# A second feed-forward product group in seven block products instead of eight, with one more buffer for raw weights

## The chip, the cores and the metric

The kernel runs on one core of a Trainium2 chip. The metric is the time of one execution on the device in microseconds (us); smaller is better. All numbers are of this one core.

## What is computed

One layer of an encoder block on 256 rows (frames) of width 1024, in float32. `rmsnorm` scales each row; every sub-layer is normed before and after and added to `x`:

```
x = x + 0.5 * rmsnorm(swiglu(rmsnorm(x, g1), Wg1, Wu1, Wd1), p1)    # feed-forward 1
h = rmsnorm(x, gm)
merged = sigmoid(h@Wga) * attention(h) + sigmoid(h@Wgb) * spatial_gating(h)
x = x + rmsnorm(merged @ Wo, pm)                                    # the mixer
x = x + 0.5 * rmsnorm(swiglu(rmsnorm(x, g2), Wg2, Wu2, Wd2), p2)    # feed-forward 2

def swiglu(h, w_gate, w_up, w_down):
    return (silu(h @ w_gate) * (h @ w_up)) @ w_down     # 1024 -> 4096 -> 1024
```

The change is about the two feed-forwards, and there about `h @ w_gate`.

## The kernel before

**Precision.** The matmuls take their operands as float32r. Each float32 weight tile `raw` is therefore split in two parts, `hi` (a cast on ACT, L88) and `lo = raw - hi` (a subtraction on DVE, L89), and so is the transposed input `xT`. A product is three matmuls for each 128 of depth: x_hi by w_hi, x_hi by w_lo, x_lo by w_hi. A weight tile has 128 x 2048 elements, 1024 KB, and is loaded by one DMA from the SP queue (L104).

**A feed-forward** (`ffn`) goes over four blocks of 1024 of the 4096 hidden columns. In a block come the gate columns `g`, then the up columns `u`. `gate_done` takes silu of a gate result on ACT into a tile `sg` (L383); `up_done` multiplies the up result into it on DVE (L390) and puts off `turn`, which transposes the 128 x 512 tile on TensorE into a bank `hp` (L398) and splits it into `hT` (L88, L89). The down products of a finished block (`down`, L377) wait in a list `side` and are strung in between the steps of the next block, eight to a block, each of 12 matmuls for the two halves of the rows.

**Two ways to make 1024 columns.** `section` needs eight block products: 4 weight tiles, each split once and used for both halves of the 256 rows. It is made in eight steps of 12 matmuls. `fast` needs seven products by a scheme of the Strassen kind: the input and the weights are cut in four quarters, sums of the quarters are multiplied, and sums of the results give the output. It has seven steps, each with one product of 12 matmuls (L301) and a weight split of its own, so seven splits. The sums of the input (`sums`, L273 and L281) are made once in a feed-forward. The sums of the weights are four per use. With `dma` false all four are DVE additions of 128 x 2048 (`add`, L305). With `dma` true two of them are made by a second transfer that adds its data onto a loaded tile (`two`: a load from SP, then an accumulating DMA from the POOL queue, L315), and two remain DVE additions; five tiles of raw weights are then loaded in place of four. Five sums of results are DVE instructions of 128 x 512 (`mixed`, L309), and one result is copied on ACT (L322).

Before, the set `FAST1` (also `FAST2`) holds the up columns of blocks 1, 2 and 3. All gate columns are made by `section`, and the up columns run with `dma` false, since `dma` is `(b, "g") in quick`. In the mixer the columns `ga` alone are made by `fast`, with `dma` true.

**Order.** The program text gives each step's instructions and calls `tick` after it; `later(n, fn)` runs `fn` at the n-th tick. A planner decides at build time, from the program's order and from its own estimate of when inputs and buffers are there, the order of the instructions on each engine and queue. On the chip each engine and queue then works strictly in that order, with semaphore waits. So a load whose buffer is free can stand far ahead of its place in the text.

**Buffers.** `raws` has 6 buffers for raw weights and gains, `wts` 4 for `hi` and 4 for `lo`, `mid` 10 of 128 x 512, `psum` 8 banks, of which four hold the down sums `ys` through a feed-forward. `mask`, `wf`, `wfs`, `ws` and `idle` are small operands of the mixer (`idle`: of the first matmuls); before, they have places of their own (`wfs` and `ws` share the pool `aux`).

Of the kernel before, what the change touches and what calls it, by code (L numbers as in the profile page):

```python
# [15 lines left out]
F32 = mybir.dt.float32  # L16
F32R = mybir.dt.float32r
# [5 lines left out]
P = 128  # L23
# [5 lines left out]
KT = D // P  # L29
H = 8  # L30
# [4 lines left out]
NB = 4  # L35
# [2 lines left out]
HOLD = 2  # L38
WARM = 14
FORGET, SCORES, TURN = 5, 3, 3  # L40
FAST1 = {(b, "u") for b in range(1, NB)}
FAST2 = FAST1
FASTM = {"ga"}

# [2 lines left out]
def block(ctx: ExitStack, tc: tile.TileContext, a: dict, out: bass.AP):  # L47
    nc = tc.nc
    const = ctx.enter_context(tc.tile_pool(name="const", bufs=1))
    raws = ctx.enter_context(tc.tile_pool(name="raws", bufs=6))  # L50
    wts = ctx.enter_context(tc.tile_pool(name="wts", bufs=4))
    mid = ctx.enter_context(tc.tile_pool(name="mid", bufs=10))
    big = ctx.enter_context(tc.tile_pool(name="big", bufs=3))
    part = ctx.enter_context(tc.tile_pool(name="part", bufs=1))
    aux = ctx.enter_context(tc.tile_pool(name="aux", bufs=1))
    small = ctx.enter_context(tc.tile_pool(name="small", bufs=4))
    psum = ctx.enter_context(tc.tile_pool(name="psum", bufs=8, space=PSUM))

# [3 lines left out]
    def mid_tile(shape, name):  # L62
        return mid.tile(shape, F32, tag="m", name=name)


    const.tile([P, 96], F32, name="pad0")
    x = const.tile([P, NT, D], F32, name="x")
    nc.sync.dma_start(out=x[:, 0, :], in_=a["x"][0])
    xT = const.tile([P, KT, NT, 2, P], F32R, name="xT")
# [55 lines left out]
    def later(n, fn):  # L125
        pending.append([n, fn])
# [158 lines left out]
    def fast(src, name, parts, done, dma):  # L285

        def get(c, kh):
            return load(src[c, kh], f"{name}{c}{kh}")

        def lhs_x(kh, t):  # L290
            return lambda k, xs: xT[:, kh * 4 + k, t, xs, :]

        def lhs_s(i):
            return lambda k, xs: parts[0][:, i, k, xs, :]

        def product(ps, lhs, raw, nm, start):
            w = parts_of(raw, f"{name}{nm}")
            for k in range(4):
                hi, lo = [z[:, k * 512:(k + 1) * 512] for z in w]
                for q, (xs, z) in enumerate(((0, hi), (0, lo), (1, hi))):  # L300
                    nc.tensor.matmul(ps, lhsT=lhs(k, xs), rhs=z, start=start and k == 0 and q == 0,  # L301
                                     stop=k == 3 and q == 2, skip_group_check=True)

        def add(out, p, q):
            nc.vector.tensor_tensor(out=out, in0=p, in1=q, op=ALU.add)  # L305

        def mixed(nm, p, q, op):
            o = mid_tile([P, 512], f"{name}{nm}")
            nc.vector.tensor_tensor(out=o, in0=p, in1=q, op=op)  # L309
            return o  # L310

        def two(first, second):

            raw = get(*first)
            nc.gpsimd.dma_start(out=raw, in_=src[second], accum_op=ALU.add)  # L315
            return raw

        b11 = get(0, 0)
        a = bank(f"{name}A")
        product(a, lhs_x(0, 0), b11, "p1", True)  # L320
        p1 = mid_tile([P, 512], f"{name}p1")
        nc.scalar.copy(out=p1, in_=a)  # L322
        yield
        if dma:
            t1 = two((1, 0), (0, 0))
        else:
            b12 = get(1, 0)
            add(b11, b11, b12)
            t1 = b11
        c = bank(f"{name}C")  # L330
        product(c, lhs_s(0), t1, "p5", True)
        yield
        b22 = get(1, 1)
        add(b11, t1, b22)
        b = bank(f"{name}B")
        product(b, lhs_s(1), b11, "p6", True)
        u2 = mixed("u2", b, p1, ALU.add)
        w = mixed("w", c, u2, ALU.subtract)
        yield
        b21 = get(0, 1)  # L340
        product(a, lhs_x(1, 0), b21, "p2", False)
        done(0, 0, a)
        add(b11, b11, b21)
        yield
        if not dma:
            add(b12, b12, b22)
        product(c, lhs_s(3), b22, "p3", False)
        done(0, 1, mixed("y01", c, u2, ALU.subtract))
        yield
        d = bank(f"{name}D")  # L350
        product(d, lhs_s(2), two((1, 0), (1, 1)) if dma else b12, "p7", True)
        done(1, 1, mixed("y11", w, d, ALU.subtract))
        yield
        product(d, lhs_x(1, 1), b11, "p4", False)
        done(1, 0, mixed("y10", d, u2, ALU.add))
        yield
# [4 lines left out]
    def ffn(n, quick, done, before=None, after=None, first=None, within=None):  # L361


        gs, us, dn = a[f"g{n}"], a[f"u{n}"], a[f"dn{n}"]
        hTs, ys, downs, sgs = {}, {}, {}, {}

        def down(f, t, cs=(0, 1)):
            if f not in downs:
# [18 lines left out]
        def up_done(b):  # L387
            def go(t, c, y):
                h = sgs[t, c]
                nc.vector.tensor_tensor(out=h, in0=y, in1=h, op=ALU.mult)  # L390

                def turn():
                    f4 = 2 * b + c
                    if f4 not in hTs:
                        hTs[f4] = big.tile([P, 4, NT, 2, P], F32R, tag="b", name=f"hT{n}_{f4}")
                    ps = bank(f"hp{n}_{b}{t}{c}")
                    for i in range(4):
                        nc.tensor.transpose(out=ps[:, i * P:(i + 1) * P], in_=h[:, i * P:(i + 1) * P], identity=ident)  # L398
                    marks[n, f4] = split(hTs[f4][:, :, t, 0, :], hTs[f4][:, :, t, 1, :],
                                         ps.rearrange("p (i c) -> p i c", c=P))[1]  # L400
                later(2, turn)
            return go

        side, parts = [], []
        for b in range(NB):
            steps = []
            for src, kind, fn in ((gs[b], "g", gate_done(b)), (us[b], "u", up_done(b))):
                nm = f"{kind}{n}_{b}"
                if (b, kind) == (0, "g"):
                    steps.append((section(src, nm, fn, first, within) if first else section_by_tile(src, nm, fn, 4), 8))  # L410
                elif (b, kind) in quick:
                    steps.append((fast(src, nm, parts, fn, (b, "g") in quick), 7))
                else:
                    steps.append((section(src, nm, fn), 8))
            total = sum(k for _, k in steps)
            keep = HOLD if b == NB - 1 else 0
            had, gone, at = len(side) - keep, 0, 0
            for gen, _ in steps:
                for _ in gen:
                    at += 1  # L420
                    if b == 0 and at == 4 and before:
                        before()
                    if b == 0 and at == 9 and quick:
                        parts.append(sums(f"f{n}"))
                    tick()
                    while had > 0 and gone < had * at // total:
                        f = side.pop(0)
                        down(f, 0)
                        down(f, 1)
                        gone += 1  # L430
            side += range(8 * b, 8 * b + 8)
# [21 lines left out]
            tick()  # L453

    def forget():
        mask = const.tile([P, P], F32, name="mask")
        nc.sync.dma_start(out=mask, in_=a["mask"])
        wf = small.tile([P, KT, H], F32, tag="wf", name="wf", bufs=1)
        nc.sync.dma_start(out=wf, in_=a["w_f"])
        bf = small.tile([H, 1], F32, tag="bf", name="bf", bufs=1)  # L460
        nc.sync.dma_start(out=bf, in_=a["b_forget"])

        wfs = aux.tile([P, KT, P], F32R, tag="aux", name="wfs")
        idr = const.tile([P, 2, P], F32R, name="idr")
        zero = const.tile([P, 1], F32, name="zero")
        pick = const.tile([P, H], F32R, name="pick")

        cs = small.tile([P, 3, P], F32R, tag="cs", name="cs", bufs=1)
        nc.vector.memset(zero, 0.0)
        with tc.issue_after(marks[1, 6].ins):  # L470
            nc.vector.tensor_copy(out=wfs, in_=zero.unsqueeze(2).broadcast_to([P, KT, P]))
            split(wfs[:, :, 0:H], wfs[:, :, 32:32 + H], wf)
            nc.vector.tensor_copy(out=idr[:, 0], in_=ident)
            nc.vector.tensor_copy(out=idr[:, 1], in_=mask)
            nc.vector.tensor_tensor(out=pick, in0=ident[:, 0:H], in1=ident[:, 32:32 + H], op=ALU.add)
            nc.vector.tensor_copy(out=cs, in_=zero.unsqueeze(2).broadcast_to([P, 3, P]))
        later(FORGET, lambda: forget_gates(wfs, bf, zero, cs))
        return cs, idr, pick
# [91 lines left out]
    def mixer(turn_in):  # L570
# [21 lines left out]
        columns(a["w_ga"], "ga", ga_done)  # L592


        ws = aux.tile([P, H, P], F32, tag="aux", name="ws")
        nc.vector.memset(ws[64:128, :, 0:64], 0.0)
        nc.sync.dma_start(out=ws[0:64], in_=a["w_s"][0:64])
        nc.sync.dma_start(out=ws[64:128, :, 64:128], in_=a["w_s"][64:128, :, 64:128])
# [76 lines left out]
        return turn  # L675


    idle = const.tile([P, 512], mybir.dt.bfloat16, name="idle")
    nc.vector.memset(idle, 0.0)
    warm = bank("warm")  # L680
    for _ in range(WARM):
# [120 lines left out]
```

## Time and profile before

| what | value |
|---|---|
| time before, median of 3 runs | 749.5 us (749.47 to 750.47) |
| the profiled execution's own time | 749.68 us |
| its span, first to last instruction | 747.9 us |
| TensorE (PE) busy | 732.6 us, 98% of the span, 3434 matmuls |
| DVE, ACT, POOL busy | 564.9, 390.4, 14.9 us |
| mean granted TensorE clock | 0.996 |

An engine's busy time is the time in which at least one of its instructions ran. PEld is TensorE's loading of the stationary operand, which overlaps its matmuls. DMA shares are shares of the core's 16 DMA engines. The profile adds 1.8 us around the span to reach the execution's own time.

### The profile page before, as it was taken

To read this page: it belongs to the slowest core of one execution; us is meant where nothing else is said; L and a number is where in the kernel's file an instruction comes from. 1 tells how busy PE (TensorE), PEld (TensorE's weight loads), DVE (VectorE), ACT (ScalarE), POOL (GpSimd) and SP (SyncE) were. 2 spreads that over 40 slices of the span, in tenths; PEclk is the share of its full clock that TensorE was granted. 3 is DMA by queue.
4 is the path that set the end of the run, shared out by engine and by line. 5 is a ranking of instruction groups with operands and counts; after the bars stand their busy time and mean duration, and the time that the engine had idled before them with its cause. 6 is when DMAs were issued, how large, how long until landed. Compare 5 with 4: busy or idle time off the path is not lost.

```text
span 747.9 us, 8563 instructions
## 1 busy us (share of the span) xinstructions
PE 732.6 (98%) x3434; PEld 605.9 (81%) x3434; DVE 564.9 (76%) x587; ACT 390.4 (52%) x406; POOL 14.9 (2%) x22
## 2 busy tenths in 40 slices
PE   7999999999999999999999999999999999999996
PEld 4888888888887877889888888878888888888785
DVE  5964798689479876769898756978489868947963
ACT  3853465456446463856774434754446435635631
POOL 0000000000000000000001000100000000000000
PEclk9999999999999999999999999999999999999999
DMA  8964167328516835873475625466417733841601
GB/s 333 393 260 174 57 230 301 143 73 341 205 57 222 322 129 192 288 200 98 166 276 212 242 96 225 139 241 240 170 59 275 285 112 126 325 168 57 250 3 57
DMA packets 23127, 144.77 MB, mean 194 GB/s; under 512 B 3312, under 2 KB 3568, under 8 KB 6576
## 3 DMA queue, kind: packets, MB, share of 16 engines
q1 hardware_dynamic: 22800, 142.13, 51.4%
q0 software_dynamic: 288, 2.10, 1.6%
q8 instruction: 27, 0.44, 0.2%
q14 instruction: 12, 0.10, 0.0%
HBM read 143.17 MB, written 1.05 MB: 193 GB/s over the span
## 4 chain that ended last, share of the span: by engine, by line
PE 89%; DVE 6%; ACT 1%; issue 1%; POOL 1%; DMA 1%; SPq 0%; POOLq 0%; DVEq 0%; ACTq 0%
PE g L225 22%; PE y L377 21%; PE u L225 9%; PE qk L204 4%; PE gb L225 3%; PE sv L225 3%; PE qk L205 2%; PE hp L398 2%; PE v L225 2%; PE u_2D L301 1%; PE u_1D L301 1%; PE wo L225 1%; PE u_3D L301 1%; PE u_1C L301 1%; PE u_2C L301 1%; PE u_2A L301 1%
## 5 line engine op out<-in xcount | busy, mean ns | idle before, releaser
L225 PE MATMUL g<-hi_g,xT 128*128 128x512 f32 x512 | 165.4, 394 | 0.7 <-ACT xT L88 0.7
L377 PE MATMUL y<-hi_d,hT 128*128 128x512 f32 x512 | 146.2, 391 | 0.0
L225 PEld LDWEIGHTS g<-hi_g,xT 128*128 128x128 f32 x512 | 96.9, 189 | 21.3 <-ACT xT L88 1.3
L377 PEld LDWEIGHTS y<-hi_d,hT 128*128 128x128 f32 x512 | 95.8, 188 | 19.6
L89 DVE TENSOR_TENSOR lo_g<-raw_g,hi_g 128x2048 fp32r<-128x2048 f32 (+1 forms) x50 | 75.0, 1519 | 41.5 <-ACT hi_g L88 41.1
L225 PE MATMUL g<-lo_g,xT 128*128 128x512 f32 x256 | 100.6, 393 | 1.1 <-DVE lo_g L89 1.1
L89 DVE TENSOR_TENSOR lo_d<-raw_d,hi_d 128x2048 fp32r<-128x2048 f32 x32 | 73.2, 2288 | 37.6 <-ACT hi_d L88 37.5
L88 ACT CAST hi_d<-raw_d 128x2048 fp32r<-128x2048 f32 x32 | 61.2, 1912 | 44.8 <-PE g L225 8.6
L377 PE MATMUL y<-lo_d,hT 128*128 128x512 f32 x256 | 80.9, 392 | 0.0
L88 ACT CAST hi_g<-raw_g 128x2048 fp32r<-128x2048 f32 (+1 forms) x50 | 62.8, 1292 | 32.3 <-PE u L225 9.3
L225 PE MATMUL u<-hi_u,xT 128*128 128x512 f32 x192 | 60.6, 391 | 0.0
L225 PEld LDWEIGHTS g<-lo_g,xT 128*128 128x128 f32 x256 | 48.5, 189 | 12.0 <-DVE lo_g L89 2.2
L305 DVE TENSOR_TENSOR raw_u<-raw_u,raw_u 128x2048 f32<-128x2048 f32 x24 | 55.0, 2292 | 0.8
L377 PEld LDWEIGHTS y<-lo_d,hT 128*128 128x128 f32 x256 | 47.8, 188 | 9.4
L383 ACT ACTIVATE sg<-g 128x512 f32<-128x512 f32 x32 | 18.8, 598 | 60.5 <-PE g L225 60.5
L204 PE MATMUL qk<-xT,hi_qk 128*128 128x512 f32 x128 | 46.5, 404 | 0.0
L225 PEld LDWEIGHTS u<-hi_u,xT 128*128 128x128 f32 x192 | 36.0, 188 | 7.4
L88 ACT CAST hi_u_3p<-raw_u 128x2048 fp32r<-128x2048 f32 x14 | 26.6, 1914 | 26.0 <-DVE raw_u L305 17.4
L89 DVE TENSOR_TENSOR lo_u_3p<-raw_u,hi_u_3p 128x2048 fp32r<-128x2048 f32 x14 | 32.0, 2287 | 9.4 <-ACT hi_u_3p L88 9.4
L225 PE MATMUL u<-lo_u,xT 128*128 128x512 f32 x96 | 37.4, 389 | 0.0
L88 ACT CAST hi_u_2p<-raw_u 128x2048 fp32r<-128x2048 f32 x14 | 26.9, 1918 | 20.1 <-DVE raw_u L305 9.5
L88 ACT CAST hi_u_1p<-raw_u 128x2048 fp32r<-128x2048 f32 x14 | 26.8, 1917 | 20.1 <-DVE raw_u L305 9.5
(289 smaller groups left out, 1292.4 us busy)
## 6 DMA issues: line engine op xcount, KB each, us to landing
raw_u<-in_u SPq DMA_DIRECT2D x32, 1024.0 KB, 4.8
raw_d<-in_dn SPq DMA_DIRECT2D x32, 1024.0 KB, 4.8
raw_g<-in_g SPq DMA_DIRECT2D x30, 1024.0 KB, 4.8
raw_qk<-in_w_qk SPq DMA_DIRECT2D x8, 1024.0 KB, 4.8
raw_ga<-in_w_ga SPq DMA_DIRECT2D x5, 1024.0 KB, 4.8
raw_v<-in_w_v SPq DMA_DIRECT2D x4, 1024.0 KB, 4.8
raw_sv<-in_w_sv SPq DMA_DIRECT2D x4, 1024.0 KB, 4.8
raw_u<-in_w_u SPq DMA_DIRECT2D x4, 1024.0 KB, 4.7
```

Source lines behind the costliest of these rows:

```text
L88: return [nc.scalar.copy(out=hi, in_=src), nc.vector.tensor_tensor(out=lo, in0=src, in1=hi.bitcast(F32), op=ALU.subtract)]
L89: nc.vector.tensor_tensor(out=lo, in0=src, in1=hi.bitcast(F32), op=ALU.subtract)]
L204: nc.tensor.matmul(ps, lhsT=hi, rhs=xT[:, k], start=k == 0, stop=False, skip_group_check=True)
L205: nc.tensor.matmul(top, lhsT=lo, rhs=xT[:, k, :, 0, :], start=False, stop=k == KT - 1, skip_group_check=True)
L225: nc.tensor.matmul(ps, lhsT=xT[:, kh * 4 + k, t, xs, :], rhs=v, start=kh == 0 and k == 0 and q == 0, stop=kh == 1 and k == 3 and q == 2)
L301: nc.tensor.matmul(ps, lhsT=lhs(k, xs), rhs=z, start=start and k == 0 and q == 0, stop=k == 3 and q == 2, skip_group_check=True)
L305: nc.vector.tensor_tensor(out=out, in0=p, in1=q, op=ALU.add)
L377: nc.tensor.matmul(ys[t][c], lhsT=hTs[f // 4][:, f % 4, t, xs, :], rhs=w[:, c * 512:(c + 1) * 512], start=f == 0 and q == 0, stop=f == NF ...
L383: nc.scalar.activation(out=sg, in_=y, func=AF.Silu)
L398: nc.tensor.transpose(out=ps[:, i * P:(i + 1) * P], in_=h[:, i * P:(i + 1) * P], identity=ident)
```

## The change

- `(2, "g")` joins the set: the gate columns of block 2 of both feed-forwards are made by `fast`. For block 2 `dma` becomes true, for the gate and for the up columns.
- `raws` has 7 buffers in place of 6, `mid` 9 in place of 10. `aux` goes; `wfs` and `ws` take a raw buffer each while they live, `mask`, `wf` and `idle` a buffer of `mid`.
- In `fast`, the third product `p3` now stands ahead of the addition `b11 + b21` and of `b12 + b22`.
- `turn` of the up results is put off by 3 ticks in place of 2 in blocks 1 and 2.
- The down products start two steps later in a block and are then spaced more closely.

```
-FAST1 = {(b, "u") for b in range(1, NB)}
+FAST1 = {(b, "u") for b in range(1, NB)} | {(2, "g")}
...
-    raws = ctx.enter_context(tc.tile_pool(name="raws", bufs=6))
+    raws = ctx.enter_context(tc.tile_pool(name="raws", bufs=7))
...
-    mid = ctx.enter_context(tc.tile_pool(name="mid", bufs=10))
+    mid = ctx.enter_context(tc.tile_pool(name="mid", bufs=9))
...
-    aux = ctx.enter_context(tc.tile_pool(name="aux", bufs=1))
...
-    const.tile([P, 96], F32, name="pad0")
+    const.tile([P, 32], F32, name="pad0")
...
         done(0, 0, a)
+        yield
+        product(c, lhs_s(3), b22, "p3", False)
         add(b11, b11, b21)
-        yield
         if not dma:
             add(b12, b12, b22)
-        product(c, lhs_s(3), b22, "p3", False)
...
+        early = [b for b in range(NB - 1) if (b, "u") in quick]
...
-                later(2, turn)
+                later(3 if b in early else 2, turn)
...
-                    while had > 0 and gone < had * at // total:
+                    while had > 0 and gone < had * max(0, at - 2) // (total - 2):
...
-        mask = const.tile([P, P], F32, name="mask")
+        mask = mid_tile([P, P], "mask")
...
-        wf = small.tile([P, KT, H], F32, tag="wf", name="wf", bufs=1)
+        wf = mid_tile([P, KT, H], "wf")
...
-        wfs = aux.tile([P, KT, P], F32R, tag="aux", name="wfs")
+        wfs = raws.tile([P, 2 * KT, P], F32R, tag="raw", name="wfs")[:, 0:KT]
...
-        ws = aux.tile([P, H, P], F32, tag="aux", name="ws")
+        ws = raws.tile([P, 2 * H, P], F32, tag="raw", name="ws")[:, 0:H]
...
-    idle = const.tile([P, 512], mybir.dt.bfloat16, name="idle")
+    idle = mid.tile([P, 512], mybir.dt.bfloat16, tag="m", name="idle")
```

## Rows read from the trace of the kernel before

**Rows 1.** The page: span, busy time of each engine

```profile
span 747.9 us, 8563 instructions
PE 732.6 (98%) x3434; PEld 605.9 (81%) x3434; DVE 564.9 (76%) x587; ACT 390.4 (52%) x406; POOL 14.9 (2%) x22
```

**Rows 2.** Chain that ended last, blocks 1 and 2: start us, us, engine, line

```profile
97.95 2.72 PE y L377 x12
...
123.88 2.73 PE g L225 x12
126.61 0.44 PE hp L398 x4
...
157.00 2.72 PE u_2A L301 x12
```

**Rows 3.** Busy time by stage: us, then PE, PEld, DVE, ACT, POOL, clock, DMA

```profile
123.88:188.35 64.47, 64.47 (x294) 53.32 (x293) 50.90 (x33) 33.53 (x24) 0.00 (x0) 1.00 0.52 195
157.00:188.00 31.00, 31.00 (x145) 25.58 (x144) 29.58 (x22) 19.28 (x13) 0.00 (x0) 1.00 0.69 264
188.35:218.75 30.40, 30.40 (x138) 25.17 (x137) 18.21 (x10) 12.22 (x10) 0.00 (x0) 1.00 0.39 142
218.00:240.00 22.00, 21.66 (x98) 17.55 (x97) 19.93 (x14) 14.04 (x9) 0.00 (x0) 1.00 0.38 133
306.00:341.00 35.00, 35.00 (x218) 31.18 (x217) 25.29 (x44) 22.09 (x39) 1.92 (x2) 1.00 0.85 249
```

**Rows 4.** Waits of PE, whole span: us in total, times, longest us

```profile
PE u_3C L301 <- DVE u_3w L309: 0.7, 2, 0.3
```

**Rows 5.** Groups by line and shape: xcount, busy us, mean ns

```profile
L89 DVE TENSOR_TENSOR lo_u_2p<-raw_u,hi_u_2p 128x2048 fp32r<-128x2048 f32 x14 | 31.9, 2289 | 1.8 <-ACT hi_u_2p L88 1.8
L88 ACT CAST hi_u_2p<-raw_u 128x2048 fp32r<-128x2048 f32 x14 | 26.9, 1918 | 20.1 <-DVE raw_u L305 9.5 <-PE u_2B L301 7.0 <-PE y L377 2.9
```

**Rows 6.** Timeline of DVE around the start of block 2

```profile
92.25 2.29 DVE L89 TENSOR_TENSOR lo_d<-raw_d,hi_d 128x2048 fp32r<-128x2048 f32 x1 [2.60 <-ACT hi_d L88]
...
113.62 2.28 DVE L89 TENSOR_TENSOR lo_g<-raw_g,hi_g 128x2048 fp32r<-128x2048 f32 x1
...
121.74 0.69 DVE L390 TENSOR_TENSOR sg<-u_1y,sg 128x512 f32<-128x512 f32 x1
122.90 2.29 DVE L89 TENSOR_TENSOR lo_g<-raw_g,hi_g 128x2048 fp32r<-128x2048 f32 x1 [0.47 <-ACT hi_g L88]
```

**Rows 7.** Timeline of DVE in the up columns of block 3

```profile
227.86 2.28 DVE L305 TENSOR_TENSOR raw_u<-raw_u,raw_u 128x2048 f32<-128x2048 f32 x1
230.06 0.69 DVE L309 TENSOR_TENSOR u_3u<-u_3B,u_3p 128x512 f32<-128x512 f32 x1
230.67 2.28 DVE L89 TENSOR_TENSOR lo_u_3p<-raw_u,hi_u_3p 128x2048 fp32r<-128x2048 f32 x1
232.87 0.69 DVE L309 TENSOR_TENSOR u_3w<-u_3C,u_3u 128x512 f32<-128x512 f32 x1
```

**Rows 8.** DMA queues and issues: packets, MB, share; KB each, us to landing

```profile
q1 hardware_dynamic: 22800, 142.13, 51.4%
q0 software_dynamic: 288, 2.10, 1.6%
...
raw_u<-in_u SPq DMA_DIRECT2D x32, 1024.0 KB, 4.8
...
raw_ga<-in_w_ga POOLq DMA_DIRECT2D x2, 1024.0 KB, 8.4
```

**Rows 9.** Timeline of POOL: the accumulating transfers of `ga`

```profile
315.72 1.05 POOL L315 DMA_DIRECT2D raw_ga<-in_w_ga  x1 [30.16 <-DMA raw_ga<-in_w_ga]
331.00 0.87 POOL L315 DMA_DIRECT2D raw_ga<-in_w_ga  x1 [14.23 <-DVE s_qk L214]
```

**Rows 10.** Timeline of the SP queue: a small operand of the mixer

```profile
58.23 0.43 SPq L457 DMA_DIRECT2D mask<-in_mask  x1
```

## The prediction

> **What bounds the kernel now.** I read the page first, then the chain of waits, then busy time by stage, then PE's own waits, then the timelines of DVE, POOL and SP around block 2. The page shows PE busy for 732.6 of 747.9 us [rows 1]. The chain shows why in the feed-forwards: it runs from one product to the next on PE, 2.72 us for each 12 matmuls, with 0.44 us for each transposed tile between them [rows 2]. By stage, block 2 of the first feed-forward lasts 64.47 us and PE is busy in all of it, while DVE has 50.90 and ACT 33.53 [rows 3]. So in that block a product less on PE is 2.72 us less, as long as nothing else becomes the last to come. PE's waits in the feed-forwards' blocks are one of 0.3 us in each, in block 3 [rows 4].
>
> **The product taken out.** Gate of block 2 goes from eight steps to seven, in each of two feed-forwards. The block had 8 + 7 + 8 = 23 steps of 2.72 and four tiles of 0.44, 64.3 us by the sum against 64.47 measured; it becomes 22 steps, 61.6 by the sum, 61.75 from the measured length. Worth 2 x 2.72 = **5.44 us**. The matmuls keep their shape, and the existing `fast` products have the same 2.72 as the section's [rows 2].
>
> **What DVE gets for it.** In a section a split serves two steps, in `fast` one: 7 splits in place of 4, so 3 more of 2.29 [rows 5], of which about 2.24 count, since neighbours overlap a little (32 or 33 instructions sum to 52.4 by their durations and to 50.90 in the window, [rows 3]). Five sums of results come in, 0.69 each and 0.61 from start to start [rows 7]. The additions of raw weights come out even: up had four on DVE, now gate and up have two each. So 50.90 + 6.7 + 3.2 = **60.8 us of DVE work in 61.75 us**, 98%. ACT gets three casts of 1.92 [rows 5] and a copy of a result (below 0.7 by its size, as the sums): 33.53 + 6.4 = 40 of 61.75, no bound.
>
> Can DVE run at 98%? The densest stretch without a PE wait is the up half of this block: 29.58 of 31.00, 95.4% [rows 3]. At that density 60.8 us of work take 63.7, which is 2.0 more than PE leaves. What hides it is the lead with which DVE enters the block: its last product of block 1 is done at 122.43, PE starts block 2 at 123.88, and the first gate split was done at 115.90 [rows 2, 6]. The new spacing puts five in place of four down steps beside block 1's up products (after steps 9, 11, 12, 14, 15), which gives DVE 2.72 us more there, so it comes about 1.45 + 2.72 = 4.2 us ahead. After the block the gate of block 3 is a section, where DVE has 18.21 of 30.40 to do [rows 3] and recovers. 4.2 covers 2.0. I therefore put no steady loss here, but an allowance for the first three steps: gate's first three products come with no down step between them, and three late `turn`s need banks of the same four that the products use, so a transposed tile's split (one 0.6 us instruction, behind at most one split of 2.29) can hold PE. The cost per block lies between 0 and 2.0 (the lead gone altogether); I take 0.6, the one small instruction, **+1.2 us** in all.
>
> **A rule against it.** The block's rows show PE busy in 64.47 of 64.47, with PEld, the loading of its stationary operand, at 53.32, 83% [rows 3]. The Trainium skill (Perfetto Trace Analysis, Identifying the Most-Contended Engine) says that matmul busy time is no good measure of TensorE's headroom, that its load time is, and that the engine with the highest share is the one to relieve. By it DVE at 98% would be the engine to relieve, and less work on PE would give nothing: the second rival below, about 747.3, where the rows give 744.6. The trace speaks for the rows as far as it goes: a chain that stays on PE through the block.
>
> **Transfers.** Each of gate and up now loads five tiles and adds two accumulating transfers: 14 loads and 4 accumulations in block 2 in place of 12 loads. A load is 2.84 us of all 16 engines (142.13 MB in 51.4% of 747.9 us; 1024 KB of it), an accumulation 6.0 (2.10 MB in 1.6%, two of them) [rows 8]. That is 39.8 + 24.0 = 63.8 us in a block of 61.75; it fits only because loads run ahead into block 1 and on into block 3, where shares are 0.39 to 0.52 [rows 3]. How far ahead: the second gate tile takes the buffer of block 1's third down tile. That one's split ended at 94.54, 3.4 us before its down product began at 97.95 [rows 2, 6]; in the new spacing this product starts 8 steps and two transposed tiles, 22.6 us, ahead of block 2. So the buffer is free at -26.0 us, the load lands after 4.8, POOL issues for 1.05, the addition lands 8.4 later [rows 8, 9]: ready at -11.7. Its split is due at -1.0 (the second product starts at +3.2; cast 1.92 and subtraction 2.29 before it). 10.7 us to spare, so nothing on the path. Behind the waiting instruction on POOL stand only the next accumulations; the norms' POOL work comes after block 3. In the mixer, `ga` has the same pattern: one POOL issue came 30.16 us after the instruction before it, at the landing of its load, and PE was busy for all 35.00 us around both, at a DMA share of 0.85 [rows 3, 9].
>
> **The third product moved ahead.** In block 3 the addition at 227.86 (2.28 us, b11 + b21) stands in front of `u_3u`, the split of the third product and `u_3w`, for which PE waits [rows 4, 7]. With the split ahead, and a fourth down step beside these products, 0.34 each should go: **-0.68 us** (bounds 0 and 0.68).
>
> **The rest, at nothing.** `turn` one step later leaves its first down product, also two steps later, one step more than before; it costs only if a bank or a `mid` buffer is short. `mask` and `wf` can take `mid` buffers as early as 58.23, where `mask` is loaded now [rows 10], and keep them to the mixer: seven of nine left in the first feed-forward, where block 2 holds at most four `sg` and three sums. The seventh raw buffer is spent on `wfs` or `ws` in the mixer (six left, as now) and is what carries the transfers above.
>
> **Sum.** 749.5 - 5.44 - 0.68 + 1.2 = **744.6 us**. The terms come from an execution of 749.68 (span 747.9), 0.2 above the median; they are small enough to be taken off the median as they are. Own range of this case: 743.4 (no allowance) to 746.5 (allowance 1.6 per block).
>
> **Rivals.**
> 1. *DVE sets the pace of block 2.* For it: 98% is above any stretch seen, and in the block 3 stretch where PE did wait DVE stood at 19.93 of 22.00, 90.6% [rows 3]. Against it: the lead. With the lead not usable and 95.4%, the block takes 63.7, 0.8 less than now: 749.5 - 1.5 - 0.7 = 747.3. At 90.6% it takes 67.1, 2.6 more: 749.5 + 5.3 - 0.7 = 754.1. It turns to a loss below 94.3% (60.8 / 64.47).
> 2. *The accumulated tile comes late* (the other side). For it: a chain of 14.25 us where a plain load has 4.8, in order on POOL, at a DMA load of a full block. Against it: 10.7 us to spare. If the buffer came free only at the split of block 1's last up product (it starts two steps and a transposed tile, 5.9 us, ahead of block 2; its split ends some 2 us before), at about -8 us, the tile were ready at +6.2, its split at +10.4 against +3.2: 7.2 us lost per block, 749.5 + 2 x (7.2 - 2.72) - 0.7 = 757.8. It decides from 10.7 + 2.7 = 13.4 us later than worked out.
> 3. *Too few `mid` buffers in the first feed-forward* (two kept by `mask` and `wf`), so only the second gains: 749.5 - 2.72 - 0.7 + 0.6 = 746.7. For it: the early load; against: the count above.
>
> **How the numbers follow.** First case 0.60. Rival 1 0.24 (0.10 faster, 0.09 within 0.2%, 0.05 slower), rival 2 0.11 (0.01 within, 0.10 slower), rival 3 0.05 (0.04 faster, 0.01 within). 0.2%, 1.5 us, is about what a measurement of this kernel tells from no change. Faster 0.74, same 0.11, slower 0.15. The range goes from 742.8, a little below the case without any allowance, to 750.5, which takes in rival 3 and the upper densities of rival 1; what is left out is below 2 in 10.
>
> **What would show it.** Right: 3410 matmuls; two steps fewer, block 2 at 61.7 to 63 us in both feed-forwards; DVE above 95% in it; PE's wait on `u_3w` gone; accumulated tiles landed 5 us or more before their split. Wrong: PE idle in block 2 ended by a `lo` split or a sum (rival 1), by a raw tile or an L315 landing (rival 2), or by `hp` and `sg` in the first feed-forward alone (rival 3).

## The result, and the profile after

The changed kernel takes 762.9 us (median of four runs, 761.8 to 764.2) against 749.75 before: ratio 1.017, interval 1.0158 to 1.0182. It is 13 us slower, where 744.6 and "faster" were forecast; the time lies outside the range. Its profiled execution took 763.53 us.

The page of the kernel after, its head and its DMA queues (queue: packets, MB, share of 16 engines):

```profile
span 761.8 us, 8586 instructions
...
PE 736.1 (97%) x3410; PEld 605.9 (80%) x3410; DVE 582.4 (76%) x603; ACT 400.7 (53%) x414; POOL 21.9 (3%) x30
...
q1 hardware_dynamic: 23376, 146.32, 51.4%
q0 software_dynamic: 1440, 10.49, 7.2%
...
raw_g<-in_g POOLq DMA_DIRECT2D x4, 1024.0 KB, 10.6
raw_u<-in_u POOLq DMA_DIRECT2D x4, 1024.0 KB, 11.6
```

The 24 matmuls are gone (3410 in place of 3434), yet PE's busy time rose from 732.6 us [rows 1] to 736.1. An accumulating transfer lands 10.6 (gate) or 11.6 us (up) after its issue, in the median of four each, where the forecast took 8.4 [rows 8].

Busy time by stage of the kernel after: blocks 1 and 2 of the first feed-forward, block 2 of the second (us, then PE, PEld, DVE, ACT, POOL, granted clock, DMA share):

```profile
59.72:124.14 64.42, 64.42 (x293) 53.43 (x292) 47.90 (x31) 31.39 (x23) 1.02 (x1) 1.00 0.51 176
124.14:195.19 71.05, 65.65 (x281) 53.00 (x280) 59.96 (x41) 40.46 (x29) 2.63 (x3) 0.95 0.81 264
596.26:666.57 70.31, 65.39 (x282) 52.85 (x280) 59.40 (x41) 40.47 (x29) 2.24 (x3) 0.95 0.82 264
```

Block 2 lasts 71.05 and 70.31 us, where it lasted 64.47 [rows 3] and should have shrunk to 61.75. Two things are new in it: PE stands still for 5.4 us (71.05 - 65.65), and PE's busy time itself is 3.9 us over 61.75, at a mean granted clock of 0.95. PE's own waits say where (us in total, times, longest):

```profile
PE u_2B L300 <- DVE lo_u_2p L88: 3.7, 2, 1.8
PE u_2B L300 <- ACT hi_u_2p L87: 3.5, 2, 1.8
...
PE g_2A L300 <- ACT hi_g_2p L87: 2.7, 2, 1.6
```

`u_2B` is the product p6 of block 2's up; PE stands still before its first and before its second matmul, right behind p5 (`u_2C`). PE's timeline there, and DVE's at the split of t1, the accumulated tile that p5 uses:

```profile
162.64 0.39 PE L300 MATMUL u_2C<-hi_u_2p,parts_f 128*128 128x512 f32 x1
164.78 0.49 PE L300 MATMUL u_2B<-hi_u_2p,parts_f 128*128 128x512 f32 x1 [1.75 <-ACT hi_u_2p L87]
167.11 0.79 PE L300 MATMUL u_2B<-lo_u_2p,parts_f 128*128 128x512 f32 x1 [1.83 <-DVE lo_u_2p L88]
```

```profile
157.71 2.29 DVE L88 TENSOR_TENSOR lo_u_2p<-raw_u,hi_u_2p 128x2048 fp32r<-128x2048 f32 x1 [4.73 <-ACT hi_u_2p L87]
```

The wait on `u_3w` of before [rows 4] is gone. The chain of waits through that place (start us, us, what):

```profile
135.18 2.21 DVE lo_d L88
137.39 0.02 issue
137.40 4.80 DMA raw_u<-in_u
...
142.73 12.94 DMA raw_u<-in_u
...
155.77 1.92 ACT hi_u_2p L87
...
159.92 0.69 DVE g_2y L308
160.60 2.21 DVE raw_u L304
162.81 0.02 issue
162.83 1.91 ACT hi_u_2p L87
164.74 0.02 issue
164.76 2.30 DVE lo_u_2p L88
167.07 0.04 issue
167.11 5.06 PE u_2B L300 x11
```

The chain is to be read upwards from the last line. PE waits for the split of p6's weights; that waits for a cast, the cast for the addition `b11 = t1 + b22`, and that addition is queued on DVE behind the split of t1 at 157.71, which waits for t1's cast and so for its accumulation (12.94 us from issue to landing). POOL could issue that only at 142.73, when t1's plain load had landed, and this load could start only when a split of a down tile gave its buffer back at 137.39, 13.3 us *after* the block had begun. The last line shows the third thing: 11 matmuls take 5.06 us, where a product of 12 took 2.72 [rows 2]. The granted clock in the stretches before, during and after that product:

```profile
164.00:167.10 3.10, 0.49 (x1) 0.19 (x1) 2.34 (x2) 3.10 (x3) 0.00 (x0) 0.84 0.98 243
167.10:172.20 5.10, 5.09 (x12) 4.02 (x13) 4.36 (x2) 3.04 (x2) 0.00 (x0) 0.50 0.77 262
172.20:175.30 3.10, 3.10 (x13) 2.49 (x13) 3.09 (x3) 1.91 (x1) 0.00 (x0) 0.88 0.40 169
```

0.50 is the lower of the clock's two levels, 1.2 GHz, right behind PE's two standstills of 1.75 and 1.83 us.

### The profile page after: what moved, and what is told of

Read it like the earlier page. It is cut to its first block, busy times and chain, and to the rows that moved or that the text cites. A ratio compares the mean times of both kernels' runs of the same rounds, so it can differ in the third digit from the quotient of the medians.

```text
span 761.8 us, 8586 instructions
## 1 busy us (share of the span) xinstructions
PE 736.1 (97%) x3410; PEld 605.9 (80%) x3410; DVE 582.4 (76%) x603; ACT 400.7 (53%) x414; POOL 21.9 (3%) x30
## 3 DMA queue, kind: packets, MB, share of 16 engines
q0 software_dynamic: 1440, 10.49, 7.2%
## 4 chain that ended last, share of the span: by engine, by line
PE 66%; DVE 13%; DMA 9%; ACT 5%; issue 4%; POOL 1%; SPq 0%; POOLq 0%; DVEq 0%; ACTq 0%
PE g L224 15%; PE y L377 14%; PE u L224 9%; DMA raw_u<-in_u 5%; DMA raw_g<-in_g 4%; PE qk L203 3%; PE gb L224 3%; PE sv L224 3%; DVE raw_u L304 2%; DVE lo_u_1p L88 2%; PE qk L204 1%; PE u_3D L300 1%; PE wo L224 1%; PE u_3C L300 1%; PE u_2D L300 1%
## 5 line engine op out<-in xcount | busy, mean ns | idle before, releaser
L224 PE MATMUL g<-hi_g,xT 128*128 128x512 f32 x384 | 125.0, 396 | 0.5 <-ACT xT L87 0.5
L224 PEld LDWEIGHTS g<-hi_g,xT 128*128 128x128 f32 x384 | 73.1, 190 | 16.3 <-ACT xT L87 1.3
L224 PE MATMUL g<-lo_g,xT 128*128 128x512 f32 x192 | 75.8, 395 | 1.1 <-DVE lo_g L88 1.1
L88 DVE TENSOR_TENSOR lo_g<-raw_g,hi_g 128x512 fp32r<-128x512 f32 (+1 forms) x42 | 56.6, 1370 | 14.3 <-ACT hi_g L87 14.1
L87 ACT CAST hi_g<-raw_g 128x512 fp32r<-128x512 f32 (+1 forms) x42 | 47.5, 1175 | 34.7 <-PE u L224 12.8
L377 PEld LDWEIGHTS y<-lo_d,hT 128*128 128x128 f32 x256 | 48.1, 189 | 11.4 <-DVE lo_d L88 1.3
L304 DVE TENSOR_TENSOR raw_u<-raw_u,raw_u 128x2048 f32<-128x2048 f32 x20 | 45.8, 2288 | 0.4
L224 PEld LDWEIGHTS g<-lo_g,xT 128*128 128x128 f32 x192 | 36.5, 190 | 9.4 <-DVE lo_g L88 2.2
L88 DVE TENSOR_TENSOR lo_u_1p<-raw_u,hi_u_1p 128x2048 fp32r<-128x2048 f32 x14 | 32.0, 2284 | 14.8 <-ACT hi_u_1p L87 14.8
L88 DVE TENSOR_TENSOR lo_u_2p<-raw_u,hi_u_2p 128x2048 fp32r<-128x2048 f32 x14 | 32.0, 2285 | 13.4 <-ACT hi_u_2p L87 13.4
L87 ACT CAST hi_g_2p<-raw_g 128x2048 fp32r<-128x2048 f32 x14 | 26.6, 1918 | 27.6 <-DVE raw_g L304 19.1
L87 ACT CAST hi_u_2p<-raw_u 128x2048 fp32r<-128x2048 f32 x14 | 26.5, 1904 | 21.2 <-DMA raw_u<-in_u 13.3
## 6 DMA issues: line engine op xcount, KB each, us to landing
raw_g<-in_g POOLq DMA_DIRECT2D x4, 1024.0 KB, 10.6
raw_u<-in_u POOLq DMA_DIRECT2D x4, 1024.0 KB, 11.6
```

Source lines behind the costliest of these rows:

```text
L87: return [nc.scalar.copy(out=hi, in_=src), nc.vector.tensor_tensor(out=lo, in0=src, in1=hi.bitcast(F32), op=ALU.subtract)]
L88: nc.vector.tensor_tensor(out=lo, in0=src, in1=hi.bitcast(F32), op=ALU.subtract)]
L224: nc.tensor.matmul(ps, lhsT=xT[:, kh * 4 + k, t, xs, :], rhs=v, start=kh == 0 and k == 0 and q == 0, stop=kh == 1 and k == 3 and q == 2)
L377: nc.tensor.matmul(ys[t][c], lhsT=hTs[f // 4][:, f % 4, t, xs, :], rhs=w[:, c * 512:(c + 1) * 512], start=f == 0 and q == 0, stop=f == NF ...
```

## The experiments

Two theories were set against each other. **T**: the accumulated tiles come too late. **V**: VectorE (DVE) is too full. All kernels are the changed one with the edit shown; `...` marks what is left out of an edit or a view, and a line number is one of the run's own kernel. e2 to e5 and e8 leave sums out and serve to measure time alone. The table has the median, the ratio to the runs of the kernel before beside it (their medians lie between 749.75 and 750.65 us) with its interval, and the length of blocks 1 and 2 together in either feed-forward in the profiled execution (from the first gate matmul of block 1 to that of block 3, read from PE's timeline). The profiled execution of e3 is its fastest (751.54 us), that of e8 its slowest (752.40), so their block lengths do not stand for their medians.

| kernel | us | ratio to before | blocks 1 + 2, us |
|---|---|---|---|
| before | 749.75 | 1 | 129.41, 129.42 |
| after | 762.89 | 1.0170 (1.0158 to 1.0182) | 135.47, 134.77 |
| e1_gate8 | 749.78 | 0.9994 (0.9985 to 1.0003) | 128.95, 128.92 |
| e2_noacc | 746.98 | 0.9959 (0.9945 to 0.9972) | 127.43, 127.40 |
| e3_noadd | 755.91 | 1.0066 (1.0044 to 1.0089) | 128.34, 131.05 |
| e4_neither | 744.80 | 0.9931 (0.9918 to 0.9945) | 126.33, 126.38 |
| e5_plain | 747.78 | 0.9969 (0.9960 to 0.9979) | 127.42, 127.45 |
| e6_alldve | 768.61 | 1.0246 (1.0231 to 1.0262) | 137.61, 137.78 |
| e7_pool | 785.65 | 1.0475 (1.0441 to 1.0509) | 148.26, 148.13 |
| e8_accgate | 749.34 | 0.9996 (0.9982 to 1.0009) | 130.08, 128.77 |
| e9_fill | 760.79 | 1.0140 (1.0125 to 1.0156) | 134.80, 133.86 |
| c1_own2 | 747.50 | 0.9965 (0.9953 to 0.9978) | 127.43, 127.47 |
| c2_own2w3 | 780.89 | 1.0421 (1.0392 to 1.0449) | 132.82, 131.33 |
| c3_own2b1 | 743.12 | 0.9909 (0.9886 to 0.9931) | 123.72, 123.76 |

**e1_gate8: the other edits alone**

```
-FAST1 = {(b, "u") for b in range(1, NB)} | {(2, "g")}
+FAST1 = {(b, "u") for b in range(1, NB)}
```

> The kernel after, but the gate of block 2 in eight products again (its up in seven, with four loads and four additions on VectorE, no accumulating transfer in block 2). Buffers, the later turn and the moved p3 stay as after. If the loss lies in the seven products of the gate and the transfers that come with them, the other edits together cost next to nothing: 748.5 to 750.5 us. If the smaller edits (ten to nine working tiles, the first step's moves, the later turn) carry part of it: 752 us or more.

749.78 us, no difference from before that can be measured. Buffers, the later `turn` and the moved p3 carry none of the loss. Blocks 1 and 2 are 0.46 us shorter, all of it in block 1, which is what one transposed tile takes (0.44 us, [rows 2]): by the later `turn` one tile fewer falls into these two blocks, and nothing is won in the whole.

**e2_noacc, e3_noadd, e4_neither: without the accumulations, without the additions, without both**

The first hunk is e2's edit, the other two are e3's, and e4 has all three.

```
-            nc.gpsimd.dma_start(out=raw, in_=src[second], accum_op=ALU.add)
+            if name == "ga":
+                nc.gpsimd.dma_start(out=raw, in_=src[second], accum_op=ALU.add)
...
-        add(b11, t1, b22)
+        if name == "ga" or not dma:
+            add(b11, t1, b22)
...
-        add(b11, b11, b21)
+        if name == "ga" or not dma:
+            add(b11, b11, b21)
```

> The kernel after without the four accumulating transfers of block 2 in each feed-forward stage's gate and up: the tiles of p5 and p7 hold one addend only, everything else is issued as after. Late transfers (theory T): both stretches without PE's work and the half-clock matmuls behind them go, 2 x (5.4 + 3.4) = 17.6 us less, so 744 to 748 us. VectorE too full (theory V): it has the same instructions to do in a block of 61.7 us, so most of the loss stays: 756 us or more. Both in part: 749 to 755 us.

> The kernel after without VectorE's two additions of raw weights in each seven-product stage of block 2 (ahead of p6 and of p4): p6 and p4 get weights that lack the second addend. VectorE has 4 x 2.3 = 9 us less to do in each block 2. Theory V: 744 to 748 us. Theory T: the accumulated tiles land as late as after, only the 2.3 us of one addition in the chain behind a landing goes per wait, at most 2 x 2 x 2.3 = 9 us with the clock's part: 754 to 760 us.

> Both left out: no accumulating transfer and no addition of raw weights in block 2. Theories T and V both: no stall in block 2, 743 to 746 us, which is what two products less per kernel can give. If it stays above 750 us, the loss lies in neither and in what is left: the order of the splits, the buffers, the later turn.

Without the accumulations 747.0, without the additions 755.9, without both 744.8. T's numbers held in the first two, and the common one in the third. Against V: with all of DVE's work and no accumulation the stalls on `u_2B` are gone. What DVE's four additions per block cost when no tile is waited for is e2 less e4, 2.2 us, 1.1 per block (c3_own2b1, below, has a block 2 without this cost). The 7 us of e3 must not be put down to DVE's load: its edit also cuts p6 loose from t1 (p6 takes the first loaded tile as it is), so it shortens just the chain shown above.

**e5_plain: a second transfer of the same size that does not add**

```
-            nc.gpsimd.dma_start(out=raw, in_=src[second], accum_op=ALU.add)
+            if name == "ga":
+                nc.gpsimd.dma_start(out=raw, in_=src[second], accum_op=ALU.add)
+            else:
+                nc.gpsimd.dma_start(out=raw, in_=src[second])
```

> The kernel after, but the second transfer of each accumulated tile of block 2 is a plain one (it writes over the first instead of adding to it, so p5 and p7 get weights that lack the first addend). Same queue, same bytes, same waits, same buffers. If the tiles are late because their buffers come free late and two transfers stand in a row: 757 to 763 us. If the accumulation itself makes the transfer long (10.6 to 13 us against about 5 us of a plain one): 746 to 751 us.

747.8 us: the same buffers, queue and bytes, and the loss is gone. The landing of the two kinds, from the DMA issues of this run, and POOL's issue for the up's first such tile:

```profile
raw_g<-in_g POOLq DMA_DIRECT2D x4, 1024.0 KB, 6.4
raw_u<-in_u POOLq DMA_DIRECT2D x4, 1024.0 KB, 6.5
...
raw_ga<-in_w_ga POOLq DMA_DIRECT2D x2, 1024.0 KB, 10.1
```

```profile
140.36 0.54 POOL L317 DMA_DIRECT2D raw_u<-in_u  x1 [19.51 <-DMA raw_u<-in_u]
```

`ga`, which still accumulates, takes 10.1; block 2's transfers, without the addition, 6.4 to 6.5, in the kernel after 10.6 to 11.6. The issue comes nearly as late as in the kernel after, 17.4 us behind the block's start (140.36 - 122.98) where it was 18.6 (142.73 - 124.14). So the late buffer alone would have been borne; the 4 to 5 us more per transfer make of it a tile that comes too late.

**e6_alldve: all sums of block 2 on DVE**

```
-                    steps.append((fast(src, nm, parts, fn, (b, "g") in quick), 7))
+                    steps.append((fast(src, nm, parts, fn, False), 7))
```

> The kernel after with all eight sums of raw weights of a block 2 on VectorE, from four plain loads per stage: no accumulating transfer. VectorE gets 4 x 2.3 = 9.1 us more in each block 2, about 70 us of work for a block of 61.7 us. Theory V (VectorE sets the pace as soon as it is over the block): 2 x (8 to 10) us of stall over the 745 us of no stall, with the clock's part 762 us or more. If its lead at the block's start and its slack behind it cover most of that: 748 to 756 us.

768.6 us: V's number. Block 2 of the first feed-forward, and ACT's timeline at one of its casts:

```profile
124.62:197.78 73.16, 66.45 (x281) 53.16 (x280) 66.87 (x44) 41.37 (x30) 0.00 (x0) 0.95 0.48 173
```

```profile
132.59 3.70 ACT L87 CAST hi_g_2p<-raw_g 128x2048 fp32r<-128x2048 f32 x2 [3.35 <-DVE raw_g L304]
```

The DMA share has dropped to 0.48 and DVE has 66.87 us to do, more than the 61.75 that PE needs. PE's longest wait (2.6 us on `g_2B` in each block 2) ends with a cast, and ACT stood idle before that cast for a sum of DVE (second fence). So V is a true limit, and 4.6 us of DVE work per stage are the price of avoiding the two accumulations in this way; but it is not what slowed the kernel after, whose DVE has two sums fewer per stage.

**e7_pool: the sums for p4 and p7 on GpSimd**

The edit of e6_alldve, and:

```
-        def add(out, p, q):
-            nc.vector.tensor_tensor(out=out, in0=p, in1=q, op=ALU.add)
+        def add(out, p, q, eng=nc.vector):
+            eng.tensor_tensor(out=out, in0=p, in1=q, op=ALU.add)
...
-        add(b11, b11, b21)
+        add(b11, b11, b21, nc.gpsimd if name.endswith("_2") else nc.vector)
...
-            add(b12, b12, b22)
+            add(b12, b12, b22, nc.gpsimd if name.endswith("_2") else nc.vector)
```

> As the run before it, but in block 2 the sums for p4 and p7 are made by GpSimd, so VectorE has just what it has in the kernel after (two sums per stage) and there are four plain loads per stage instead of five with two accumulating transfers. Theory T: without accumulating transfers the stalls go, 745 to 749 us, faster than before. Theory V: 755 us or more. A third way: GpSimd's sums are long (5 us or more each) or hold up VectorE's own while they run; then p4 or p7 waits: 752 to 760 us.

785.7 us: T's number failed, and so did the third way's upper bound of 760, though DVE held up by GpSimd is what the trace shows. The timelines of GpSimd (first line) and of DVE (the others) in one place of block 2:

```profile
136.04 4.61 POOL L304 TENSOR_TENSOR raw_g<-raw_g,raw_g 128x2048 f32<-128x2048 f32 x1 [9.47 <-DVE lo_g_2p L88]
```

```profile
136.48 6.32 DVE L88 TENSOR_TENSOR lo_g_2p<-raw_g,hi_g_2p 128x2048 fp32r<-128x2048 f32 x1
142.72 2.28 DVE L88 TENSOR_TENSOR lo_d<-raw_d,hi_d 128x2048 fp32r<-128x2048 f32 x1
```

GpSimd adds from 136.04 to 140.65. The split that DVE begins at 136.48 takes 6.32 us, not 2.28: what is left of GpSimd's addition (4.17) and then its own length, 6.45 by the sum. It stood still until GpSimd was done. In the four places of this block DVE's instruction beside such a sum is 2.7 to 4.4 us longer than its like elsewhere. The Trainium skill (SBUF — State Buffer, SBUF: two separate sides) says that the two engines share a pair of ports that one instruction holds for its whole length, and that a DVE instruction with two SBUF inputs is locked out by a GpSimd one that reads SBUF. This trace agrees, with 6.32 us in place of 2.28. A sum moved to GpSimd therefore costs DVE more here than the 2.3 us of making it itself.

**e8_accgate: the accumulations of the gate alone**

```
-            nc.gpsimd.dma_start(out=raw, in_=src[second], accum_op=ALU.add)
+            if name[0] == "g":
+                nc.gpsimd.dma_start(out=raw, in_=src[second], accum_op=ALU.add)
```

> The kernel after with the accumulating transfers of block 2's gate, but without those of its up (p5 and p7 of the up get one addend only). If the up's tiles, of which the chain of waits names the longest, cause most: 748 to 752 us. If the gate's transfers set off the loss (everything behind them on VectorE and ScalarE is late, too): 755 us or more.

749.3 us. Without the up's accumulations the kernel after is 13.6 us faster. The gate's cost about 2.4 us (749.3 against 747.0 without any), and their wait is PE's longest in this run:

```profile
PE g_2A L300 <- ACT hi_g_2p L87: 3.7, 2, 2.0
```

**e9_fill: PE kept at work in the stall**

```
+        kept = [None, None]
...
+            if nm == "p6" and name[0] == "u" and name.endswith("_2"):
+                for i in range(8):
+                    nc.tensor.matmul(ps, lhsT=lhs(0, 0), rhs=kept[0][:, 0:512], start=True, stop=True,
+                                     skip_group_check=True)
...
+            kept[:] = w
```

> The kernel after with eight more matmuls (3.1 us, of values that the next start overwrites) on PE just ahead of p6 of block 2's up, where PE stands still for 3.6 us in all. The stall itself stays as long; only PE is kept at work in it. If the half clock behind the stall (the 11 matmuls of p6 take 5.06 us instead of 2.72, and some more at a granted clock of 0.84 to 0.88) is a consequence of PE's idle time: 2 x 3.4 = 6.8 us less, about 756 us. If the clock falls for another reason, or the added matmuls come to stand behind the stall: 763 to 769 us.

760.8 us: 2 us less where 6.8 were expected. PE's timeline at p6 and at the up's last step, and busy time by stage, of the stretch between the two and of the whole block 2, in this run:

```profile
162.29 1.98 PE L300 MATMUL u_2B<-hi_u_2p,parts_f 128*128 128x512 f32 x8
164.11 0.39 PE L307 MATMUL u_2B<-hi_u_2p,parts_f 128*128 128x512 f32 x1
166.25 0.50 PE L307 MATMUL u_2B<-lo_u_2p,parts_f 128*128 128x512 f32 x1 [1.75 <-DVE lo_u_2p L88]
...
187.55 0.47 PE L307 MATMUL u_2D<-hi_u_2p,xT 128*128 128x512 f32 x1 [1.71 <-DVE u_2y L315]
```

```profile
163.91:187.55 23.64, 20.18 (x90) 16.11 (x89) 23.64 (x16) 15.33 (x9) 0.00 (x0) 1.00 0.89 325
123.23:193.61 70.38, 64.72 (x290) 52.48 (x288) 61.53 (x43) 40.37 (x29) 2.62 (x3) 1.00 0.85 279
```

The clock's part of the expectation came true: with only one standstill left (1.75 us; the added matmuls filled 1.8 of 3.6), the granted clock stays at 1.00. PE's busy time, 64.72 us with the 1.8 of added matmuls in it, is 2.8 below that of the kernel after. But PE then runs into a new wait of 1.7 us at `u_2D`, for a result sum of DVE. The last fence's first line tells why: from the late split on, DVE is busy for 23.64 of 23.64 us. It had stood idle 4.4 us for the accumulated tile, and in a block that it nearly fills there is no place to make them up. In the kernel after there is no wait at `u_2D`: there the slow p6 seems to have hidden this second queue.

**c1_own2: two buffers of their own for the accumulated tiles**

```
-    raws = ctx.enter_context(tc.tile_pool(name="raws", bufs=7))
+    raws = ctx.enter_context(tc.tile_pool(name="raws", bufs=5))
+    acc = ctx.enter_context(tc.tile_pool(name="acc", bufs=2))
...
-            raw = get(*first)
+            if name.endswith("_2"):
+                raw = acc.tile([P, 2048], F32, tag="acc", name=f"acc_{name}{first[0]}{first[1]}{second[0]}")
+                nc.sync.dma_start(out=raw, in_=src[first])
+            else:
+                raw = get(*first)
```

> The kernel after with two buffers of their own for the accumulated tiles of block 2, and five raw buffers for all else instead of seven shared ones: the first load of the up's p5 tile can then go as soon as the gate's p5 tile is split, about 28 us before it is due, where load and accumulation need 5 + 13 = 18 us. Theory T (late by the chain load, accumulation, split, not by the transfers' sum): the stalls in block 2 go, 746 to 750 us, if five buffers do for the rest. If the rest needs six or seven: its waits come in other places, 752 us or more. If the transfers' sum (DMA engines full, accumulation at 6.0 us of engine time per MB) sets it: 758 us or more.

747.5 us, faster than both kernels, at the same number of buffers. The accumulations are not shorter on the whole (gate 11.4 against 10.6, up 9.8 against 11.6); they start earlier. POOL's timeline, and the landing times:

```profile
130.87 0.88 POOL L319 DMA_DIRECT2D acc_u<-in_u  x1 [62.06 <-ACT hT L88]
151.81 0.88 POOL L319 DMA_DIRECT2D acc_u<-in_u  x1 [20.06 <-DMA acc_u<-in_u]
```

```profile
acc_g<-in_g POOLq DMA_DIRECT2D x4, 1024.0 KB, 11.4
...
acc_u<-in_u POOLq DMA_DIRECT2D x4, 1024.0 KB, 9.8
```

The up's first accumulation is issued 7.4 us after the block's start (130.87 - 123.42), not 18.6 (142.73 - 124.14). So the sum of the transfers, with the same accumulations, is not what sets the loss. In block 2 of this run PE is busy in 62.34 of 63.01 us and DVE in 58.45.

**c2_own2w3: the space taken from the split weights instead**

```
+    acc = ctx.enter_context(tc.tile_pool(name="acc", bufs=2))
-    wts = ctx.enter_context(tc.tile_pool(name="wts", bufs=4))
+    wts = ctx.enter_context(tc.tile_pool(name="wts", bufs=3))
```

The accumulated tiles come from `acc`, as in c1_own2; `raws` stays at 7.

> The same two own buffers, with all seven raw buffers kept and the space taken from the split weights (three pairs of hi and lo instead of four). Theory T as before: no stall by transfers in block 2. The split weights' lead falls from three products to two, so VectorE's bursts (98% busy in block 2) show sooner: 747 to 752 us if a lead of 5.4 us does, 755 us or more if not.

780.9 us, the expectation's case "755 us or more", and far beyond that bound. Little of it lies in block 2: in the first feed-forward that lasts 64.08 us, but block 1 68.74, and from block 3 to the second feed-forward it is 309.4 us where it was 288.6 before. PE's waits in this run include 4.4 us in the mixer and 1.6 on `u_3w` in each feed-forward. The kernel needs the fourth pair of split weights nearly everywhere; raw buffers it can spare.

**c3_own2b1: block 1's gate in seven products as well**

The edit of c1_own2, and:

```
-FAST1 = {(b, "u") for b in range(1, NB)} | {(2, "g")}
+FAST1 = {(b, "u") for b in range(1, NB)} | {(1, "g"), (2, "g")}
...
-            if name.endswith("_2"):
+            if name[-2:] in ("_1", "_2"):
```

> The kernel with two own buffers for accumulated tiles (the 747.5 us one), and the gate of block 1 in seven products too, its and its up's p5 and p7 tiles accumulated in the same two buffers: two more products less, and eight more accumulating transfers in the kernel. If a block in which VectorE has 98% to do costs nothing as long as the tiles are there, as block 2 in the run before: 2 x 2 us less, 743 to 745 us. If VectorE's lead pays for one such block alone (its work of 60.8 us was measured as 58.5 inside the block of 63.0, the rest done ahead), the second one stalls: 748 to 756 us. If the accumulating transfers of two blocks in a row (8 x 6.0 us of engine time) are too many: its waits end at their landing, 752 us or more.

743.1 us, 0.9909 of before (0.9886 to 0.9931). Blocks 1 and 2 of the first feed-forward, then block 1 and 2 of the second:

```profile
62.03:123.87 61.84, 61.84 (x282) 51.03 (x280) 56.71 (x39) 37.53 (x27) 3.50 (x4) 1.00 0.89 288
123.87:185.75 61.88, 61.88 (x282) 51.13 (x280) 58.00 (x41) 40.69 (x29) 3.50 (x4) 1.00 0.90 304
521.98:583.81 61.83, 61.83 (x281) 51.01 (x280) 56.72 (x39) 37.54 (x27) 3.52 (x4) 1.00 0.88 282
583.81:645.74 61.93, 61.93 (x282) 51.11 (x280) 58.00 (x41) 40.67 (x29) 1.73 (x2) 1.00 0.81 264
```

Four blocks at 61.8 to 61.9 us, close to the forecast's 61.75, with PE busy in all of it, DVE in 92 to 94% of it and the DMA engines in 0.81 to 0.90. Only the entry into block 1 of the first feed-forward is later, 62.03 us against 59.00 in c1_own2, and PE waits there for 2.6 us at a transposed tile in block 0, a wait that c1_own2 doesn't have. Block 2 does the same additions here as in c1_own2, where it lasts 63.01 us and PE waits 0.45 us in its gate's first products; DVE begins the gate's first addition 2.3 us ahead of the block here (121.61 against 123.87) and 0.1 in c1_own2 (123.29 against 123.42). So the additions need not cost anything; that their place makes the difference was not tested by itself.

## Why the prediction was wrong

**The product taken out (-5.44): right.** 3410 matmuls, and a block that is not held up lasts 61.84 to 61.93 us (c3_own2b1), 61.75 forecast.

**DVE's work (60.8 of 61.75): right, and bearable.** In a block 2 without late tiles DVE shows 58.0 to 58.5 us (c3_own2b1, c1_own2), since some splits run ahead; the sign "DVE above 95%" was therefore not met by any of them (94% at most). The allowance of 0.6 per block was near: e2 less e4 makes it 1.1, c3_own2b1 nothing. Rival 1 is not what happened, but its limit is real: with 66.9 us of DVE work (e6) the block takes 73.16 us. The rule of the Trainium skill (Perfetto Trace Analysis, Identifying the Most-Contended Engine), read by load time alone as the prediction read it, would have relieved DVE first; c3_own2b1 does not bear it out, for there DVE's share is above PEld's 83% and less work on PE still shortened each block to PE's own length. Beside load time that rule of the Trainium skill names the arithmetic done as a share of the peak, which the prediction left out and no row here gives.

**The transfers: the step that failed.** "10.7 us to spare, so nothing on the path" put the late tile at nothing, and its working was wrong in three ways.
- *Only the gate's first accumulated tile was worked out.* That one came at -6.1 us instead of -11.7 (issued at 105.18, 12.86 us to its landing) and cost little (e8: both gate tiles, 1.2 us per block). The up's was never worked out. The down tile whose buffer it inherits is split inside block 2, so its load began at +13.3 us, and it landed at +31.5.
- *The accumulation was priced by a lone pair in the mixer, 8.4 us.* In block 2, with the DMA engines full (0.81 over the block, 1.00 in its middle), it took up to 13.0. That the loss needs this length, e5 shows: the same transfer without the addition lands in 6.5, and the loss is gone. That it needs the late buffer too, c1 shows: with a longer lead it is gone at the full length. Neither does it alone.
- *The due time was taken from the tile's own split.* But p6's addition reads the tile as well: from landing to p6's last operand the chain runs 11.4 us (155.67 to 167.07), and p6 stands right behind p5 on PE, with no down step between them.

Rival 2 was the right mechanism, "the accumulated tile comes late", with a chance of 0.11 and 757.8 us. It laid the lateness on the gate's tile, where the up's made most of it, and it was under-sized: it had 7.2 us lost per block, where PE stood still for 5.4 and 4.9 and was busy for 3.9 and 3.6 longer. That second part it did not count: the granted clock falls to 0.50 behind the stall, and in e9, without that, PE's busy time is 2.8 of the 3.9 lower. Nor can DVE make up the 4.7 us that it stands idle for the tile; e9 shows the wait that comes of it once the clock stays up.

**The moved p3 (-0.68): the wait went, the gain can't be told.** `u_3w` is off the list of waits in every run but c2_own2w3, and e1, which has this edit without the gate's, is 0.9994 of before with 1 in the interval.

**The rest at nothing: right** (e1). `hp` and `sg` showed no wait in the kernel after; rival 3 did not occur.

One point stays open: why an accumulating transfer takes 4 to 5 us longer than a plain one of the same size. The engines' own time per MB is higher (10.49 MB take 7.2% of the span with the additions and 4.5% in e5), but which part of it is the addition and which the wait among other loads was not separated. Full DMA engines alone do not explain the longest ones: in c3_own2b1, with shares of 0.81 to 0.90 over the blocks, the medians are 9.3 and 9.9.

## What to carry to other kernels

When a change adds an operation in several places, work out the slack of each place, the last one first: the first instance inherits a lead that the later ones do not have. A stall in a block whose second engine is nearly full can be worth more than its own length: here 5.4 us of standstill became 9.3 us by the clock, and without the clock's part DVE had no room to make up what it had waited. Before giving up a scheme because its transfers are slow, give them buffers that come free early: here the same long transfers, started 11 us sooner, turned a loss of 13 us into a gain of 2.8, and then let a second block follow.

## What the runs showed of the hardware

- An accumulating DMA of 1 MB from the POOL queue landed after 8.4 (before) to 12.0 us (e3) beside other loads, by the medians of runs and tiles, single ones after up to 13.2; the same without the addition after 6.4 to 6.5 (e5).
- PE's granted clock was 0.50 for one product (5.06 us for 11 matmuls) right behind two standstills of 1.75 and 1.83 us that lay one matmul apart. Behind a single standstill it went either way: it stayed at 1.00 behind 1.75 and 1.97 us (e9) and 2.57 (c3), and fell to 0.55 behind 1.95 (e8, over the next 2 us) and to 0.51 behind 2.98 (e3, over the next 3.2). So the length of a standstill alone does not tell.
- A GpSimd addition of 128 x 2048 took 4.61 us (three of four in a block of e7; 6.58 the fourth), and a DVE subtraction on two SBUF tiles that began beside it ended only after it (6.32 us in place of 2.28).
